# The second expert handled is always number 1, with token groups of 4, 2, 2 tiles and features in natural order

## The chip, the cores and the metric

The kernel runs on one core of one Trainium2 chip. The core has five engines that work side by side, each on its own list of instructions: TensorE (PE, with its weight loads shown apart as PEld), VectorE (DVE), ScalarE (ACT), GpSimd (POOL) and SyncE (SP), which here issues most DMAs. The metric is the device time of one execution in microseconds (us), the median of several runs.

## What is computed

One layer of a decoder with 1024 tokens of 1024 features: two attentions that share an input projection, a cross-attention to a memory of 256 rows, and a mixture of 16 experts in 4 groups of 4. Only the end of it is changed, so only that stands here:

```python
x = x + MemoryCrossAttention(RMSNorm(x), mem)
h = RMSNorm(x)                                    # gain moe_norm_g
g_sel = argmax(softmax(h @ w_group))              # one of 4 groups
aff = sigmoid(h @ w_expert) of that group         # 4 affinities
local = top_k(aff + expert_bias, 2)               # two experts of the group
w_sel = p_group * a_sel / sum(a_sel)
for e in range(16):
    act = silu(h @ w_gate[e]) * (h @ w_up[e])
    y = y + combine[:, e] * (act @ w_down[e])
x = x + y
```

Each token goes to two experts, so the 16 experts have 2048 tokens in all, unevenly spread.

## The kernel before

Tokens lie in 8 tiles of 128. The tiles of `x` stay in SBUF (`xres`), with eight more columns per token for weights, expert number and token number. `Memory.step` runs the memory attention as a pipeline over the tiles, beside the last half of the product with `w_out`: `E` adds the attention to `x`, `F` normalizes the tile for the experts (two ScalarE scalings L482, one VectorE product with the gain L484 that also reorders the features), `G` ends the router's logits and calls `Route.step`.

`Route.group` routes four tiles at a time in some 40 small VectorE steps. Its result is a place in a table in DRAM for each token and each of its two experts; a GpSimd indirect DMA (L197) then scatters 128 rows of 1032 floats to the table `d_xs`, eight DMAs per group. So there are two groups, of tiles 0 to 3 and 4 to 7. The table has 1280 rows for each expert.

Experts are handled in an order of ranks. Expert 0 has rank 0. After the first group, `Route.lead` finds the expert with most tokens so far (the lead, rank 1) and the one with least (rank 15); their numbers are written to `nb`, and L1669 loads both into registers of SP, before the loads of the lead's weights. The first 128 rows of expert 0 and of the lead are computed early: `lift` sets the base of these two for the second group to at least 128, so that their first 128 rows are complete after the first group. After the second group, `Route.places` sorts the other experts by tokens into ranks 2 to 14.

Each rank has a fixed number of rows, its room, for which the program is written out:

```python
ORDER_ = (0, 1, 15, 2, 8, 3, 9, 4, 10, 5, 11, 6, 12, 7, 13, 14)
ROOM = 2 * (256,) + 2 * (224,) + 2 * (192,) + 2 * (160,) + 5 * (128,) + 3 * (96,)
```

`ORDER_` is the order in which ranks are handled. For each, `moe` gathers the rows (L1682), transposes them on TensorE (L1718), loads the weights (gate and up L1733, down L1756), splits each into a high and a low part (L1747, L1748), multiplies, and adds the result to the output with an indirect DMA that skips rows without a token (L1765). `places` also counts, per rank, the blocks of 128 rows beyond the room (`cb`, in `nb[32:48]`) and their sum (`nb[48]`). At the end all engines load that sum (L1903) and, where it is over zero (L1904), run loops over the ranks (L1914) with an inner loop over the blocks beyond the room (L1917): these gather the rows, load that expert's weights again and multiply in plain f32.

The order of instructions on each engine comes from a scheduler in the build; DMAs of one queue start in its order. `issue_after` in the code holds an instruction behind another in that order.

The lines are those of the profile:

Of the kernel before, what the change touches and what calls it, by code (L numbers as in the profile page):

```python
# [22 lines left out]
NE = 16  # L23
# [9 lines left out]
class Route:  # L33
# [3 lines left out]


    GROUPS = ((0, 4), (4, 8))

    def __init__(self, K, rt, rows):
        self.K, self.rt = K, rt
        nc = K.nc
        V, G = nc.vector, nc.gpsimd
        til = lambda sh, nm, dt=F32: rt.tile(sh, dt, name=nm)
        self.til = til
        self.lg = til([128, T, 20], "lg")
        self.bias = K.row('moe_expert_bias', 0, 16, "e_bias", rt)
# [19 lines left out]
        self.base = til([128, 3, 16], "base")  # L68
        G.tensor_scalar(self.base[:, 0], self.iot, float(EXP), None, op0=OP.mult)

        self.lift = til([128, 16], "lift")
        G.tensor_copy(self.lift, self.base[:, 0])
        G.memset(self.lift[:, 0:1], 128.0)
        self.nb = til([1, 64], "nb", I32)
        self.todo, self.hold, self.puts, self.late = [], False, [], []

    def step(self, t):
        for a, b in self.GROUPS:
            if t == b - 1:
                self.todo.append(self.group(a, b))  # L80
        if t == T - 1:
            self.hold = False
            self.pump(10 ** 6)
# [9 lines left out]

    def group(self, t0, t1):
        K, til0 = self.K, self.til
# [4 lines left out]
        def til(sh, nm, dt=F32):  # L100
            return self.rt.tile(sh, dt, name=nm)
# [82 lines left out]

        pos, tmp, pc, ix = til([128, n, 16], "pos"), til([128, n, 2, 16], "tmp16"), til([128, n, 2], "pc"), til([128, n, 2], "ix", I32)
        V.tensor_add(pos, pre[:, 0:w].rearrange("p (t e) -> p t e", e=16), self.base[:, t0 // 4:t0 // 4 + 1].to_broadcast([128, n, 16]))
        yield
# [3 lines left out]
        yield  # L191
        self.last_ix = V.tensor_copy(ix, pc)
        yield

        for t in range(n):
            for z in range(2):
# [4 lines left out]
                if t0 >= EARLY:  # L201
                    self.late.append(q)
        V.tensor_add(self.base[:, t1 // 4], self.base[:, t0 // 4], pre[:, 128:144])
        if t1 == LEAD_AT:
            self.lead()
        if t1 == EARLY:
            V.tensor_tensor(self.base[:, t1 // 4], self.base[:, t1 // 4], self.lift, op=OP.max)

    def lead(self):
# [3 lines left out]
        own, e = til([128, 2, 16], "lown"), til([128, 2], "le")  # L213
        V.tensor_sub(key, self.base[:, LEAD_AT // 4], self.base[:, 0])
        V.scalar_tensor_tensor(key, key, 16.0, self.w16, op0=OP.mult, op1=OP.add)
        for i, (far, op) in enumerate(((-1.0, OP.max), (65536.0, OP.min))):
            V.tensor_scalar(key[:, 0:1], key[:, 0:1], 0.0, far, op0=OP.mult, op1=OP.add)
            V.tensor_reduce(m, key, AX.X, op)
            V.tensor_scalar(own[:, i], key, m, None, op0=OP.is_equal)
            V.tensor_mul(num, own[:, i], self.iot)  # L220
            V.tensor_reduce(e[:, i:i + 1], num, AX.X, OP.add)
        V.tensor_copy(self.nb[:, 0:2], e[0:1])
        self.le = e
        V.scalar_tensor_tensor(self.lift, own[:, 0], 128.0, self.lift, op0=OP.mult, op1=OP.add)
        self.shift = til([128, 16], "lshift")
        V.tensor_sub(self.shift, own[:, 0], own[:, 1])

    def places(self, lp):
# [4 lines left out]
        key, cnt = til([128, 16], "key"), self.til([128, 16], "cnt")  # L233
        V.tensor_sub(cnt, self.base[:, T // 4], self.base[:, 0])
# [32 lines left out]
class Memory:  # L267
# [6 lines left out]
    def __init__(u, K, x, mc, wq, quarter, route, cl):  # L274
# [28 lines left out]

        u.g_o = mc.tile([128, D], F32, name="g_o")
        for h in range(2):
            raw = K.wraw.tile([128, 512], F32, name="wr")
            src = I['moe_norm_g']
            nc.sync.dma_start(raw, bass.AP(tensor=src.tensor, offset=src.offset + 512 * h, ap=[[0, 128], [1, 512]]))
            G.tensor_copy(u.g_o.rearrange("p (c i) -> p c i", c=8)[:, :, 64 * h:64 * h + 64], raw.rearrange("p (i c) -> p c i", c=8))
        u.wor, u.wr0 = mc.tile([128, 2, 2, 20], F32R, name="w_o_router"), wr  # L310
# [188 lines left out]
class Hybrid:  # L499
# [41 lines left out]

    def newton(self, v, shape):

        nc, n = self.nc, shape[-1]
        s, y, t = (self.sm.tile([128, 17], dt, name=nm)[:, :n] for nm, dt in (("rq_s", I32), ("rq_y", F32), ("rq_t", F32)))
        nc.vector.tensor_scalar_add(v, v, EPS)
        nc.vector.tensor_scalar(s, v.bitcast(I32), 1, None, op0=OP.logical_shift_right)
# [1106 lines left out]
    def moe(self, route):  # L1654
# [13 lines left out]
        nb = route.nb  # L1668
        lead = [nc.values_load(nb[0:1, i:i + 1], engines=SP, min_val=0, max_val=NE - 1) for i in range(2)]  # L1669
        flat = lambda p, nm, dt=F32: p.tile([128, 2048], dt, name=nm)  # L1670
# [25 lines left out]
        def rows_of(loaded, exf, eT, early=False):  # L1696
# [139 lines left out]
        hB = early(1, lead[0], route.le[:, 0:1])  # L1836
        xg_ = [flat(r1, f"xg{i}") for i in range(2)]

        expert, loaded = [0, lead[0], lead[1]], {}

# [8 lines left out]
        def tokens(k):  # L1851
            n, exf = loaded[k][0], (0.0, route.le[:, 0:1])[k] if k < 2 else route.ex[:, ORDER_[k]:ORDER_[k] + 1]
# [45 lines left out]
        with ExitStack() as c:  # L1898
# [5 lines left out]
            with tc.If(nov > 0):  # L1904
# [7 lines left out]
                for a, b, room in runs:  # L1912
                    r = room // 128
                    with tc.For_i(a, b, 1) as s_:  # L1914
                        ne = nc.values_load(nb[0:1, ds(s_ + 32, 1)], min_val=0, max_val=9 - r)
                        ex = nc.values_load(nb[0:1, ds(s_ + 16, 1)], min_val=0, max_val=NE - 1)
                        with tc.For_i(0, ne, 1) as k:  # L1917
# [20 lines left out]
                            for h in range(2):  # L1938
                                p = self.tp().rearrange("p (a b) -> p a b", a=4)
                                for i in range(4):  # L1940
                                    nc.tensor.transpose(p[:, i, :], g0[:, tk(4 * h + i)], self.ident)
                                V.tensor_copy(gT[:, 4 * h:4 * h + 4], p)
# [53 lines left out]
```

## Time and profile before

| what | value |
|---|---|
| median of 3 runs | 1391.09 us (1387.9 to 1392.69) |
| the profiled execution's own time | 1394.23 us |
| its span, first to last instruction | 1392.5 us |
| mean granted clock of TensorE, share of full | 0.951 |
| busy: PE, DVE, ACT, POOL | 1233.7, 954.7, 792.9, 412.1 us |
| chain that ended last, by engine | PE 44%, DVE 19%, ACT 13%, DMA 13%, issue 7% |

Busy is the time in which an engine executes; the chain is followed back from the last instruction through what released each step. Shares over the whole span mix stages with different limits. The memory attention and router end at about 1108 us, the experts take the rest.

### The profile page before, as it was taken

To read this page: it belongs to the slowest core of one execution; us is meant where nothing else is said; L and a number is where in the kernel's file an instruction comes from. 1 tells how busy PE (TensorE), PEld (TensorE's weight loads), DVE (VectorE), ACT (ScalarE), POOL (GpSimd) and SP (SyncE) were. 2 spreads that over 40 slices of the span, in tenths; PEclk is the share of its full clock that TensorE was granted. 3 is DMA by queue.
4 is the path that set the end of the run, shared out by engine and by line. 5 is a ranking of instruction groups with operands and counts; after the bars stand their busy time and mean duration, and the time that the engine had idled before them with its cause. 6 is when DMAs were issued, how large, how long until landed. Compare 5 with 4: busy or idle time off the path is not lost.

```text
span 1392.5 us, 20692 instructions
## 1 busy us (share of the span) xinstructions
PE 1233.7 (89%) x6852; PEld 1032.6 (74%) x6853; DVE 954.7 (69%) x1983; ACT 792.9 (57%) x1651; POOL 412.1 (30%) x521
## 2 busy tenths in 40 slices
PE   3998999998899999999988999999989378999894
PEld 2877778777687778787777777887878256888772
DVE  6886956899999488878978465132367735677661
ACT  4654656887662477779988221043455335676652
POOL 4565100648774010011333222021223431011111
PEclk9999999999899999999999999998999689999987
DMA  7565003543435445345221244431121757899972
GB/s 206 159 199 148 12 24 101 163 131 124 135 116 174 151 133 185 139 167 164 65 82 55 83 136 126 174 86 38 34 78 73 286 215 232 272 344 299 284 219 37
DMA packets 145558, 203.55 MB, mean 146 GB/s; under 512 B 69632, under 2 KB 90880, under 8 KB 145440
## 3 DMA queue, kind: packets, MB, share of 16 engines
q1 hardware_dynamic: 134944, 172.57, 38.5%
q0 software_dynamic: 7440, 24.71, 6.6%
q10 hardware_dynamic: 3056, 4.84, 0.9%
q8 instruction: 56, 0.92, 0.3%
q14 instruction: 62, 0.51, 0.1%
HBM read 134.61 MB, written 69.70 MB: 147 GB/s over the span
## 4 chain that ended last, share of the span: by engine, by line
PE 44%; DVE 19%; ACT 13%; DMA 13%; issue 7%; POOL 2%; SPq 1%; DVEq 0%; ACTq 0%; POOLq 0%
PE acc L530 6%; PE acc L532 5%; PE acc L531 5%; PE s L530 3%; PE s L531 3%; PE s L532 3%; DMA gu_raw<-in_moe_w_gate_dram 2%; DMA gu_raw<-in_moe_w_up_dram 2%; ACT tk_junka L1222 2%; DVE ik_hi L1212 2%; PE s L955 2%; DVE ik_lo L1212 2%; DMA out_dram<-ey,etok 2%; PE tp L1378 1%; DVE PT_lo L517 1%
## 5 line engine op out<-in xcount | busy, mean ns | idle before, releaser
L522 POOL TENSOR_TENSOR wl<-wr,wh 128x512 fp32r<-128x512 f32 (+1 forms) x78 | 101.5, 1319 | 166.5 <-ACT wh L521 125.2
L517 DVE TENSOR_TENSOR PT_lo<-tp,PT_hi 128x512 fp32r<-128x512 f32 (+1 forms) x152 | 96.9, 656 | 23.3 <-ACT PT_hi L516 21.7
L530 PE MATMUL s<-hT_hi,wh 128*128 128x512 f32 x256 | 103.5, 404 | 3.4 <-ACT s L1083 3.4
L532 PE MATMUL s<-hT_hi,wl 128*128 128x512 f32 x256 | 102.8, 403 | 1.7 <-POOL wl L522 1.7
L531 PE MATMUL s<-hT_lo,wh 128*128 128x512 f32 x256 | 102.4, 402 | 0.0
L1765 POOL DMA_INDIRECT out_dram<-ey,etok x24 | 39.4, 1642 | 207.2 <-ACT ey L1780 57.3
L1748 DVE TENSOR_TENSOR gu_lo<-gu_raw,gu_hi 128x1024 fp32r<-128x1024 f32 x60 | 71.8, 1221 | 40.3 <-ACT gu_hi L1747 39.7
L516 ACT ACTIVATE PT_hi<-tp 128x512 fp32r<-128x512 f32 (+1 forms) x152 | 83.5, 572 | 23.4 <-PE tp L1378 9.8
L1222 ACT ACTIVATE tk_junka<-sc,tk_b 128x512 bf16<-128x512 f32 (+2 forms) x96 | 79.4, 827 | 30.5 <-DVE tk_b L1219 29.6
L521 ACT ACTIVATE wh<-wr 128x512 fp32r<-128x512 f32 (+1 forms) x78 | 46.7, 619 | 73.9 <-PE acc L532 26.7
L1747 ACT ACTIVATE gu_hi<-gu_raw 128x1024 fp32r<-128x1024 f32 x60 | 62.2, 1057 | 45.5 <-DMA gu_raw<-in_moe_w_gate_dram 21.9
L532 PE MATMUL acc<-wh,hT_lo 128*128 128x512 f32 (+2 forms) x240 | 85.5, 356 | 0.4 <-DVE hT_lo L517 0.4
L530 PE MATMUL acc<-wh,hT_hi 128*128 128x512 f32 (+2 forms) x240 | 85.3, 356 | 0.3 <-ACT hT_hi L516 0.2
L531 PE MATMUL acc<-wl,hT_hi 128*128 128x512 f32 (+2 forms) x240 | 84.3, 352 | 0.0
L1358 DVE TENSOR_REDUCE low<-s 128x1 f32<-128x256 f32 (+3 forms) x64 | 49.0, 769 | 21.3 <-PE s L1357 20.9
L530 PE MATMUL s<-eT1h,gu_hi 128*128 128x224 f32 (+2 forms) x192 | 54.0, 281 | 8.0 <-DVE ewt L1711 3.9
L530 PEld LDWEIGHTS s<-hT_hi,wh 128*128 128x128 f32 x256 | 49.8, 195 | 13.9 <-ACT s L1083 4.2
L532 PEld LDWEIGHTS s<-hT_hi,wl 128*128 128x128 f32 x256 | 49.9, 195 | 12.0 <-POOL wl L522 2.1
L964 DVE SCALAR_TENSOR_TENSOR sc<-rel,iw,sc 128x384 f32<-128x384 f32 (+5 forms) x42 | 43.4, 1034 | 21.2 <-ACT rel L958 18.0
L531 PEld LDWEIGHTS s<-hT_lo,wh 128*128 128x128 f32 x256 | 50.0, 195 | 10.4
L1360 ACT ACTIVATE P<-s,low 128x256 f32<-128x256 f32 (+3 forms) x64 | 48.1, 752 | 11.9 <-DVE low L1358 9.1
L530 PE MATMUL acc<-wh,mg_hi 128*128 128x512 f32 x128 | 52.0, 411 | 3.1 <-issue 3.1
(549 smaller groups left out, 4093.6 us busy)
## 6 DMA issues: line engine op xcount, KB each, us to landing
d_xs<-zero SPq DMA_DIRECT2D x32, 516.0 KB
dn_raw<-in_moe_w_down_dram SPq DMA_DIRECT2D x32, 512.0 KB
gu_raw<-in_moe_w_gate_dram SPq DMA_DIRECT2D x30, 512.0 KB
gu_raw<-in_moe_w_up_dram SPq DMA_DIRECT2D x30, 512.0 KB
wr<-in_w_in_dram SPq DMA_DIRECT2D x48, 256.0 KB
d_g<-s SPq DMA_DIRECT2D x32, 256.0 KB
gt<-d_g SPq DMA_DIRECT2D x16, 512.0 KB
xg<-d_xs SPq DMA_DIRECT2D x13, 512.0 KB
```

What stands on the lines that cost most here:

```text
L516: q = self.nc.scalar.activation(hi, src, AF.Copy)
L517: self.nc.vector.tensor_sub(lo, src, hi.bitcast(F32))
L522: self.nc.gpsimd.tensor_sub(lo, src, hi.bitcast(F32))
L530: mm(out, a[0], b[0], start=start, stop=False)
L531: mm(out, a[0], b[1], start=False, stop=False)
L532: mm(out, a[1], b[0], start=False, stop=stop)
L1212: V.tensor_scalar(junks[0][:, :(t + 1) * 128], blk(t), b[:, i:i + 1].bitcast(F32), None, op0=op, op1=OP.add, accum_out=cnt[:, i:i + 1])
L1222: A.activation(junka[:, :(t + 1) * 128], blk(t), AF.Sign, bias=b[:, i:i + 1].bitcast(F32), accum_out=cnt[:, i:i + 1])
L1358: nc.vector.tensor_reduce(low[:, b:b + 1], sp[:, 0:nch, 0:w], AX.XY, OP.min)
L1360: nc.scalar.activation(p_[:, :Wd].rearrange("p (a b) -> p a b", a=nch), sp[:, 0:nch, 0:w], AF.Exp, bias=low[:, b:b + 1], scale=-1.0, accum ...
L1747: A.activation(hi[:, z], raw_z, AF.Copy)
L1748: E.tensor_sub(lo[:, z], raw_z, hi[:, z].bitcast(F32))
```

## The change

The second expert handled is number 1, whatever the router finds; its weights' addresses are constants, so their loads need no register. `lead` now finds only the expert with least tokens, experts 0 and 1 apart. `places` gives expert 1 rank 1 by adding 65536 to its key. The room of each rank and the order of ranks are as before. Routing goes in three groups, of four, two and two tiles. The normalized rows keep the features in natural order: `F` is one VectorE instruction with the gain row as it lies in DRAM, and the transposes of the gathered rows pick every eighth feature. The reciprocal root of tiles 6 and 7 is made by Newton steps on VectorE (12 instructions) in place of GpSimd's power.

```diff
-    GROUPS = ((0, 4), (4, 8))
+    GROUPS = ((0, 4), (4, 6), (6, 8))
...
-        G.memset(self.lift[:, 0:1], 128.0)
+        for e in range(2):
+            G.memset(self.lift[:, e:e + 1], float(e * EXP + 128))
...
-        for i, (far, op) in enumerate(((-1.0, OP.max), (65536.0, OP.min))):
-            V.tensor_scalar(key[:, 0:1], key[:, 0:1], 0.0, far, op0=OP.mult, op1=OP.add)
-            V.tensor_reduce(m, key, AX.X, op)
...
+        V.tensor_scalar(key[:, 0:2], key[:, 0:2], 0.0, 65536.0, op0=OP.mult, op1=OP.add)
+        V.tensor_reduce(m, key, AX.X, OP.min)
...
-        V.tensor_scalar(key[:, 0:1], key[:, 0:1], 131072.0, None, op0=OP.add)
-        V.scalar_tensor_tensor(key, self.shift, 65536.0, key, op0=OP.mult, op1=OP.add)
+        for e in range(2):
+            V.tensor_scalar(key[:, e:e + 1], key[:, e:e + 1], 131072.0 - 65536.0 * e, None, op0=OP.add)
+        V.scalar_tensor_tensor(key, self.own, -65536.0, key, op0=OP.mult, op1=OP.add)
...
-        u.g_o = mc.tile([128, D], F32, name="g_o")
-        for h in range(2):
...
-            G.tensor_copy(u.g_o.rearrange("p (c i) -> p c i", c=8)[:, :, 64 * h:64 * h + 64], raw.rearrange("p (i c) -> p c i", c=8))
+        u.g_o = K.row('moe_norm_g', 0, D, "g_o", mc)
...
-        K.rsqrt(u.d.pop(('ms2', t)), (128, 1), out=y)
-        xn = u.ap.tile([128, D], F32, name="mxn", bufs=1)
-        for h in range(2):
-            m = slice(512 * h, 512 * h + 512)
-            nc.scalar.activation(xn[:, m], u.x[:, t, m], AF.Copy, scale=y)
-        nat = lambda v: v.rearrange("p (i c) -> p c i", c=8)
-        nc.vector.tensor_mul(u.x[:, t, 0:D].rearrange("p (c i) -> p c i", c=8), nat(xn), u.g_o.rearrange("p (c i) -> p c i", c=8))
+        (K.newton if t >= 6 else K.rsqrt)(u.d.pop(('ms2', t)), (128, 1), out=y)
+        xt = u.x[:, t, 0:D]
+        nc.vector.scalar_tensor_tensor(xt, xt, y, u.g_o, op0=OP.mult, op1=OP.mult)
...
-                x = xg[0:m, b // 128].rearrange("p (c i) -> p c i", c=KD)
+                x = xg[0:m, b // 128].rearrange("p (i c) -> p c i", c=KD)
...
-                            for q in (route.last_act, route.last_ix):
+                            for q in (route.last_act, route.last_ix[-1]) if h else route.last_ix[-2:-1]:
...
-        gu1 = gate_up(1, lead[0], (0,), V) + gate_up(1, lead[0], (1,), V)
+        gu1 = gate_up(1, 1, (0, 1), V)
...
-        dn1 = down(1, lead[0])
+        dn1 = down(1, 1)
+        expert.append(nc.values_load(nb[0:1, 1:2], engines=SP, min_val=0, max_val=NE - 1))
```

On SP, at the end of the memory attention, the queue before loads expert 0's down weights (`dn_raw`), then the register from `nb`, then the lead's gate and up weights (`gu_raw`), then the early rows (`d_xs`):

```order
L1756 DMA dn_raw<-in_moe_w_down_dram 128x1024 x2
L1669 TENSOR_LOAD nb
L1669 ISA x2
L1669 TENSOR_LOAD nb
L1669 ISA x2
L1733 ISA
L1733 DMA gu_raw<-in_moe_w_gate_dram 128x1024
L1733 ISA
L1733 DMA gu_raw<-in_moe_w_up_dram 128x1024
```

and the same place now:

```order
L1745 DMA dn_raw<-in_moe_w_down_dram 128x1024 x2
L1722 DMA gu_raw<-in_moe_w_gate_dram 128x1024
L1722 DMA gu_raw<-in_moe_w_up_dram 128x1024
L1722 DMA gu_raw<-in_moe_w_gate_dram 128x1024
L1722 DMA gu_raw<-in_moe_w_up_dram 128x1024
L1847 TENSOR_LOAD nb
L1847 ISA x2
L1722 ISA
L1722 DMA gu_raw<-in_moe_w_gate_dram 128x1024
L1722 ISA
L1722 DMA gu_raw<-in_moe_w_up_dram 128x1024
L1671 DMA dn_raw<-d_xs 128x1024
```

The second expert's four gate and up loads stand ahead of the register load; behind it comes the first half of the third expert's.

On POOL, at the end of the router, the roots of the tiles' mean squares (`mms` to `my`) and the scatters (`d_xs`) stand before as

```order
L538 TENSOR_SCALAR mms_11237<-mms_11237 128x1
L539 TENSOR_TENSOR my_11322<-mms_11237,mhalf 128x1
L197 DMA d_xs<-xres,ix 20480x1032 x8
L538 TENSOR_SCALAR mms_11318<-mms_11318 128x1
L538 TENSOR_SCALAR mms_11393<-mms_11393 128x1
L539 TENSOR_TENSOR my_11400<-mms_11318,mhalf 128x1
L539 TENSOR_TENSOR my_11447<-mms_11393,mhalf 128x1
```

and the same place now, where the last four scatters follow after the small MEMSETs of `room`, as the last eight did before:

```order
L527 TENSOR_SCALAR mms_11101<-mms_11101 128x1
L528 TENSOR_TENSOR my_11228<-mms_11101,mhalf 128x1
L527 TENSOR_SCALAR mms_11221<-mms_11221 128x1
L528 TENSOR_TENSOR my_11303<-mms_11221,mhalf 128x1
L198 DMA d_xs<-xres,ix_11341 20480x1032 x8
L198 DMA d_xs<-xres,ix_11515 20480x1032 x4
```

The roots of the last two tiles are gone from behind the first eight scatters, and four scatters of the second group stand there.

On DVE, between the second group's places (`ix`) and the last group's first steps, there stands now

```order
L193 CAST ix_11515<-pc 128x4
L1737 TENSOR_TENSOR gu_lo_11679<-gu_raw,gu_hi_11678 128x1024 x2
L541 SCALAR_TENSOR_TENSOR rq_t<-rq_t,mms_11371 128x1
L542 SCALAR_TENSOR_TENSOR my_11458<-rq_t,my_11458 128x1
L484 TENSOR_SCALAR lg<-lg,my_11458 128x20
L473 SCALAR_TENSOR_TENSOR xres<-xres,my_11458,g_o 128x1024
L111 TENSOR_REDUCE mx<-lg 128x2
```

Two splits of the second expert's weights (`gu_lo`) stand ahead of the end of tile 7's Newton steps; before, all four stood behind the last cast to `ix`.

## Rows read from the trace of the kernel before

**Rows 1.** Busy time by engine in four stretches; then PEclk, DMA share, GB/s.

```profile
1083.00:1108.00 25.00, 6.03 (x42) 5.17 (x42) 16.39 (x73) 9.23 (x15) 10.32 (x44) 0.63 0.88 328
1108.00:1131.00 23.00, 16.08 (x63) 12.12 (x61) 10.47 (x25) 5.38 (x8) 13.72 (x19) 0.80 0.89 332
1090.00:1100.00 10.00, 0.00 (x0) 0.00 (x0) 5.01 (x19) 4.81 (x8) 4.15 (x7) 0.50 1.01 382
1160.00:1260.00 100.00, 92.92 (x584) 79.36 (x583) 69.34 (x134) 67.25 (x104) 15.93 (x10) 0.97 0.94 307
```

**Rows 2.** Chain of waits, 1060 to 1140 us: start us, us, what.

```profile
1083.27 1.13 POOL d_xs L197
...
1108.05 1.79 POOL d_xs L197
...
1118.79 12.12 DMA d_xs<-xres,ix
...
1131.51 3.53 DMA emore<-d_xs
...
1135.36 1.94 PE tp L1718 x8
```

**Rows 3.** VectorE in order of time: start, us, instruction, idle before and releaser.

```profile
1094.50 0.23 DVE L495 TENSOR_SCALAR lg<-lg,my 128x20 f32<-128x20 f32 x1 [5.75 <-POOL mms L538]
```

**Rows 4.** Queue of loads in order of time, 1085 to 1134 us.

```profile
1088.23 0.70 SPq L1733 DMA_DIRECT2D gu_raw<-in_moe_w_gate_dram  x1
...
1103.90 0.34 SPq L1682 DMA_DIRECT2D dn_raw<-d_xs  x1
```

**Rows 5.** Instructions of L482, L484, L1748: ns min/median/max, first and last start us.

```profile
L482 ACT ACTIVATE mxn<-xres,my x16: 706/710/724, 1027.1 to 1099.1; 128x512 f32<-128x512 f32 x16
...
L484 DVE TENSOR_TENSOR xres<-mxn,g_o x8: 1908/2048/3157, 1029.1 to 1101.4; 128x1024 f32<-128x1024 f32 x8
...
L1748 DVE TENSOR_TENSOR gu_lo<-gu_raw,gu_hi x60: 1208/1219/1228, 1107.7 to 1352.7; 128x1024 fp32r<-128x1024 f32 x60
```

**Rows 6.** The same of L1718, weight loads of the row transposes.

```profile
L1718 PEld LDWEIGHTS tp<-ident,xg x176: 133/140/231, 1135.3 to 1347.7; 128*128 128x128 f32 x104, 96*128 96x128 f32 x40, 64*128 64x128 f32 x16, 32*128 32x128 f32 x16
```

**Rows 7.** DMA queue q0, four stretches: 1159.85-1171.14, 1179.72-1192.17, 1362.84-1369.81, 1369.81-1373.78 us. Packets, MB, share.

```profile
q0 software_dynamic: 144, 0.45, 20.3%
...
q0 software_dynamic: 144, 0.39, 16.1%
...
q0 software_dynamic: 144, 0.52, 49.7%
...
q0 software_dynamic: 48, 0.01, 2.0%
```

**Rows 8.** Instructions of the tail, L1903, L1904, L1991: ns min/median/max, starts.

```profile
L1903 DVEq TENSOR_LOAD <-nb x1: 541/541/541, 1370.4 to 1370.4; - x1
...
L1904 PEldq EVENT_SEMAPHORE  x2: 51/51/51, 1375.0 to 1375.2; - x2
...
L1904 POOLq COMPARE_BRANCH  x1: 53/53/53, 1380.9 to 1380.9; - x1
...
L1904 POOLq EVENT_SEMAPHORE  x6: 17/30/43, 1383.8 to 1385.6; - x6
...
L1904 POOLq INC_SWDGE_SEM  x1: 1291/1291/1291, 1385.7 to 1385.7; - x1
...
L1991 POOLq EVENT_SEMAPHORE  x4: 17/17/17, 1391.7 to 1392.4; - x4
...
L1991 POOLq DRAIN  x3: 46/103/4568, 1387.1 to 1392.2; - x3
```

**Rows 9.** L1765, the adding scatters: us from issue to landing.

```profile
DMA to landing us min/median/max: 3.2/7.4/10.7
```

**Rows 10.** Chain of waits, 1050 to 1060 us: plain f32 matmuls.

```profile
1055.62 1.44 PE acc L461 x12
```

**Rows 11.** ScalarE in order of time, 1119 to 1123 us.

```profile
1119.52 1.28 ACT L1806 ACT_TABLE_LOAD   x1
```

More of the change, by code (lines that the diff above doesn't have):

```diff
@@ L66, in __init__ @@
         G.memset(self.onesb, 1.0)
-        self.base = til([128, 3, 16], "base")
+        self.base = til([128, len(self.GROUPS) + 1, 16], "base")
         G.tensor_scalar(self.base[:, 0], self.iot, float(EXP), None, op0=OP.mult)
@@ L72, in __init__ @@
         G.tensor_copy(self.lift, self.base[:, 0])
-        G.memset(self.lift[:, 0:1], 128.0)
+        for e in range(2):
+            G.memset(self.lift[:, e:e + 1], float(e * EXP + 128))
         self.nb = til([1, 64], "nb", I32)
-        self.todo, self.hold, self.puts, self.late = [], False, [], []
+        self.todo, self.hold, self.puts, self.late, self.last_ix = [], False, [], [], []
     def step(self, t):
-        for a, b in self.GROUPS:
+        for i, (a, b) in enumerate(self.GROUPS):
             if t == b - 1:
-                self.todo.append(self.group(a, b))
+                self.todo.append(self.group(i, a, b))
         if t == T - 1:
@@ L92, in pump, with group @@
             self.hold = r == 2 and n < 10 ** 5
-    def group(self, t0, t1):
+    def group(self, gi, t0, t1):
         K, til0 = self.K, self.til
@@ L100, in til @@
         def til(sh, nm, dt=F32):
-            return self.rt.tile(sh, dt, name=nm)
+            return self.rt.tile([128, 4, *sh[2:]], dt, name=nm)[:, 0:n]
+        base = self.base
         l4, l16 = self.lg[:, t0:t1, 0:4], self.lg[:, t0:t1, 4:20]
@@ L183, in group @@
         yield
-        pos, tmp, pc, ix = til([128, n, 16], "pos"), til([128, n, 2, 16], "tmp16"), til([128, n, 2], "pc"), til([128, n, 2], "ix", I32)
-        V.tensor_add(pos, pre[:, 0:w].rearrange("p (t e) -> p t e", e=16), self.base[:, t0 // 4:t0 // 4 + 1].to_broadcast([128, n, 16]))
+        pos, tmp, pc, ix = til([128, n, 16], "pos"), til([128, n, 2, 16], "tmp16"), til([128, n, 2], "pc"), til([128, n, 2], f"ix{gi}", I32)
+        V.tensor_add(pos, pre[:, 0:w].rearrange("p (t e) -> p t e", e=16), base[:, gi:gi + 1].to_broadcast([128, n, 16]))
         yield
@@ L191, in group @@
         yield
-        self.last_ix = V.tensor_copy(ix, pc)
+        self.last_ix.append(V.tensor_copy(ix, pc))
         yield
@@ L202, in group, with lead @@
                     self.late.append(q)
-        V.tensor_add(self.base[:, t1 // 4], self.base[:, t0 // 4], pre[:, 128:144])
+        V.tensor_add(base[:, gi + 1], base[:, gi], pre[:, 128:144])
         if t1 == LEAD_AT:
-            self.lead()
+            self.lead(base[:, gi + 1])
         if t1 == EARLY:
-            V.tensor_tensor(self.base[:, t1 // 4], self.base[:, t1 // 4], self.lift, op=OP.max)
-    def lead(self):
+            V.tensor_tensor(base[:, gi + 1], base[:, gi + 1], self.lift, op=OP.max)
+    def lead(self, upto):
         V, til = self.K.nc.vector, self.til
         key, m, num = til([128, 16], "lkey"), til([128, 1], "lmx"), til([128, 16], "lnum")
-        own, e = til([128, 2, 16], "lown"), til([128, 2], "le")
-        V.tensor_sub(key, self.base[:, LEAD_AT // 4], self.base[:, 0])
+        self.own, e = til([128, 16], "lown"), til([128, 1], "le")
+        V.tensor_sub(key, upto, self.base[:, 0])
         V.scalar_tensor_tensor(key, key, 16.0, self.w16, op0=OP.mult, op1=OP.add)
-        for i, (far, op) in enumerate(((-1.0, OP.max), (65536.0, OP.min))):
-            V.tensor_scalar(key[:, 0:1], key[:, 0:1], 0.0, far, op0=OP.mult, op1=OP.add)
-            V.tensor_reduce(m, key, AX.X, op)
[L219 to L226, printed above, removed]
+        V.tensor_scalar(key[:, 0:2], key[:, 0:2], 0.0, 65536.0, op0=OP.mult, op1=OP.add)
+        V.tensor_reduce(m, key, AX.X, OP.min)
+        V.tensor_scalar(self.own, key, m, None, op0=OP.is_equal)
+        V.tensor_mul(num, self.own, self.iot)
+        V.tensor_reduce(e, num, AX.X, OP.add)
+        V.tensor_copy(self.nb[:, 1:2], e[0:1])
     def places(self, lp):
@@ L233, in places @@
         key, cnt = til([128, 16], "key"), self.til([128, 16], "cnt")
-        V.tensor_sub(cnt, self.base[:, T // 4], self.base[:, 0])
+        V.tensor_sub(cnt, self.base[:, len(self.GROUPS)], self.base[:, 0])
         V.scalar_tensor_tensor(key, cnt, 16.0, self.w16, op0=OP.mult, op1=OP.add)
-        V.tensor_scalar(key[:, 0:1], key[:, 0:1], 131072.0, None, op0=OP.add)
-        V.scalar_tensor_tensor(key, self.shift, 65536.0, key, op0=OP.mult, op1=OP.add)
+        for e in range(2):
+            V.tensor_scalar(key[:, e:e + 1], key[:, e:e + 1], 131072.0 - 65536.0 * e, None, op0=OP.add)
+        V.scalar_tensor_tensor(key, self.own, -65536.0, key, op0=OP.mult, op1=OP.add)
         gt, oh, ex = (til([128, 16, 16], nm) for nm in ("gt", "oh", "ex"))
@@ L302, in __init__ @@
             G.tensor_add(u.two, u.two, K.ident[0:40, 20 * e:20 * e + 20])
-        u.g_o = mc.tile([128, D], F32, name="g_o")
-        for h in range(2):
-            raw = K.wraw.tile([128, 512], F32, name="wr")
-            src = I['moe_norm_g']
-            nc.sync.dma_start(raw, bass.AP(tensor=src.tensor, offset=src.offset + 512 * h, ap=[[0, 128], [1, 512]]))
-            G.tensor_copy(u.g_o.rearrange("p (c i) -> p c i", c=8)[:, :, 64 * h:64 * h + 64], raw.rearrange("p (i c) -> p c i", c=8))
+        u.g_o = K.row('moe_norm_g', 0, D, "g_o", mc)
         u.wor, u.wr0 = mc.tile([128, 2, 2, 20], F32R, name="w_o_router"), wr
@@ L540, in rsqrt, with newton @@
         return y
-    def newton(self, v, shape):
+    def newton(self, v, shape, out=None):
         nc, n = self.nc, shape[-1]
         s, y, t = (self.sm.tile([128, 17], dt, name=nm)[:, :n] for nm, dt in (("rq_s", I32), ("rq_y", F32), ("rq_t", F32)))
+        y = y if out is None else out
         nc.vector.tensor_scalar_add(v, v, EPS)
@@ L1668, in moe @@
         nb = route.nb
-        lead = [nc.values_load(nb[0:1, i:i + 1], engines=SP, min_val=0, max_val=NE - 1) for i in range(2)]
         flat = lambda p, nm, dt=F32: p.tile([128, 2048], dt, name=nm)
@@ L1833, in moe @@
         dn = down(0, 0)
-        gu1 = gate_up(1, lead[0], (0,), V) + gate_up(1, lead[0], (1,), V)
+        gu1 = gate_up(1, 1, (0, 1), V)
         hA = early(0, 0, 0.0)
-        hB = early(1, lead[0], route.le[:, 0:1])
+        hB = early(1, 1, 1.0)
         xg_ = [flat(r1, f"xg{i}") for i in range(2)]
-        expert, loaded = [0, lead[0], lead[1]], {}
+        expert, loaded = [0, 1], {}
         def load(k):
@@ L1851, in tokens @@
         def tokens(k):
-            n, exf = loaded[k][0], (0.0, route.le[:, 0:1])[k] if k < 2 else route.ex[:, ORDER_[k]:ORDER_[k] + 1]
+            n, exf = loaded[k][0], float(k) if k < 2 else route.ex[:, ORDER_[k]:ORDER_[k] + 1]
             return n, rows_of(loaded[k], exf, [cut(w, n) for w in eT[k % 2]])
         rest = first_small(128, gu, hA)
-        dn1 = down(1, lead[0])
+        dn1 = down(1, 1)
+        expert.append(nc.values_load(nb[0:1, 1:2], engines=SP, min_val=0, max_val=NE - 1))
         nb = route.places(r3)
@@ L1940, in moe @@
                                 for i in range(4):
-                                    nc.tensor.transpose(p[:, i, :], g0[:, tk(4 * h + i)], self.ident)
+                                    nc.tensor.transpose(p[:, i, :], g0[:, 0:D].rearrange("p (i c) -> p c i", c=KD)[:, 4 * h + i], self.ident)
                                 V.tensor_copy(gT[:, 4 * h:4 * h + 4], p)
```

## The prediction

> **What bounds the kernel now.** I read the busy times of stretches first. They show one hole. From 1083 to 1108 us TensorE is busy 6.0 us of 25, at a mean granted clock of 0.63, and from 1108 to 1131 16.1 us of 23, while the DMA engines are at shares of 0.88 and 0.89 [rows 1]. Later, from 1160 to 1260, TensorE is busy 92.9 us of 100 with the DMA share at 0.94: two resources near their limits, little to win. Next the chain of waits, for what the hole is made of: the first scatter of token rows at 1083.27, the first of the second eight at 1108.05, the last at 1118.79, landed 12.12 us later, a gather of 3.53 us, transposes at 1135.36 [rows 2]. So the path there is router, scatter, landing, gather. Then the engines' order of time. `VectorE` stands idle 5.75 us before 1094.50, because the rsqrt of the last two tiles is on GpSimd behind eight scatters [rows 3]. On the queue of loads the second expert's gate and up weights start at 1088.23, as its number is computed from the first four tiles, and the early gather starts at 1103.90 [rows 4]. Last I read the tail, because the program ends in a block for experts with more tokens than room that the kernel before skips (L1904). That block decides this forecast.
>
> **The router stage.** By rows 1 the 48 us from 1083 to 1131 move 25 x 328 + 23 x 332 GB/s = 15.8 MB. The second expert's gate and up weights, four DMAs of 0.52 MB or 2.1 MB, leave that stretch: they now follow the first expert's loads, ahead of the register load that waited for the router. At the stretch's own rate that is 2.1/0.33 = 6.4 us; where all the holes closed too (13.7 MB at the 382 GB/s of its best 10 us [rows 1], 36 us), 12 us. The last two tiles' rsqrt goes to VectorE, 24 instructions as small as the one in rows 3, 0.2 us each, among the router's, against the wait of 5.75 us. The second group's scatters are cut in two: four start behind the first eight, so only four, not eight, follow the router's last result: the first and the eighth start 10.74 us apart [rows 2], so four steps of 1.5 us, 6 us, go. But two gu_lo instructions of 1.22 us [rows 5] now stand on VectorE ahead of the last group, and behind them queue all its router steps. These gains overlap, since the bytes still have to flow. I take -10 us, bounds -3 (only the four scatters' issue, less the two gu_lo) and -18 (wait, issue and bytes all on the path). What is late next is the landing of the last four scatters, then the gather of 3.53 us.
>
> **Natural order of features.** Per tile two ScalarE scalings of 0.71 us and a strided VectorE multiply of 2.05 us become one contiguous VectorE instruction; nearest row, two f32 inputs of 128x1024: 1.22 us [rows 5]. That is 1.42 + 2.05 - 1.22 = 2.25 us per tile. Eight tiles give 18 us of engine time, mostly beside TensorE's work in the memory attention. I take -3, little more than one tile's share for the stretch ahead of the first scatter; bounds 0 (all covered) and -5 (two tiles). In return the 192 transposes of gathered rows (176, and 16 of the early blocks) read weights 8 floats apart. The trace has no such load: now one takes 140 ns [rows 6]. VectorE's ratio in rows 5, 2.05/1.22 = 1.7, would make it 100 ns longer, and at most 192 x 0.10 = 19 us; the load runs beside matmuls, so the lower bound is 0. I take +3, near the lower, as TensorE's transposes are spread over the DMA-bound stage. The Trainium skill ("SBUF — State Buffer", in "Door 1: The DMA port swizzle") says consecutive accesses are at full bandwidth only within one 16-byte line, so a stride of 32 bytes pays on each access. Rows 5 agree for VectorE; by that rule on every transpose the term would be 19 us instead of 3.
>
> The rest I cost at nothing: the counting base with one more slot, and the lead search with one branch instead of two are VectorE instructions of 0.2 us on 16 columns, hidden by the scatters; the two strided gain copies on GpSimd fall in the w_out stage, where it waits. Uncovered they are 2 us, of either sign.
>
> **The overflow.** Each rank in the order of handling has fixed rows, `ROOM`: 256, 256, 224, 224, 192, 192, 160, 160, five times 128, three times 96. What an expert has beyond is done by the block at the end. The trace gives each expert's tokens, because the adding DMA moves a row of 4096 bytes for each real token [rows 7]. In order: the lead's early block 0.45 MB and its second 0.39 MB, about 110 + 96 = 206 rows; the expert at rank 7 0.52 + 0.01 MB, 128 + 2. Working the reference's routing out on its inputs gives the same: number 2 (now the lead) 206, number 7 130, number 1 only 79. Now number 1 gets rank 1 and its room of 256, number 2 joins the sorted ranks at the front, and every expert between moves down one. Number 7 comes from rank 7, room 160, to rank 8, room 128, with 130 tokens. Two tokens overflow, `nov` is 1, and all five engines enter the block. All others fit (206 and 189 in 224; 179 and 157 in 192; 154 and 139 in 160; 127 in 128).
>
> The block has six loops with 16 turns in all over the ranks, one of them with an inner turn. A turn holds register loads (0.54 us each, two on VectorE), a compare, a chain of 12 semaphore waits (51 ns each on TensorE's queue), updates of the DMA semaphores on GpSimd, and between turns a drain and two barriers. No loop ran before, so I bound a turn by the end rows [rows 8]. Cheap: 1.1 + 0.6 + 0.8 for the barriers (the end block takes 0.8 us behind its drain) + branches, some 2.9 us. Dear: also two updates of 1.29 us, a GpSimd drain of 4.57 us and two taken jumps of 2.9 us (GpSimd's compare at 1380.9, its next instruction at 1383.8): 15.5 us. I take 6 us, nearer the cheap end, as the loops' code is short. 16 x 6 = 96 us, bounds 46 and 248.
>
> The inner turn is one serial chain: five small VectorE steps 1; zeroing scatter to landing 7.4 [rows 9]; 3.1 MB of weights at 307 GB/s [rows 1] 10.2, with the gather beside them; 32 plain f32 matmuls at twice 0.12 us [rows 10], since the granted clock is 0.50 while TensorE idles [rows 1], 7.7; table load 1.28 [rows 11] and two small steps, 2.1; four matmuls of 512 columns 3.8; two ScalarE copies 1.4; the adding scatter 7.4. Sum 41 us; bounds 27 (full clock, landings of 3.2) and 48 (landings of 10.7).
>
> The Trainium skill ("Runtime: NRT & Kernel Launch", "Instruction fetch mechanics") says a taken branch stalls only where its target lies outside the two instruction pages held, which trigger a fetch. The far jump in rows 8 agrees, 2.9 us on GpSimd; the short jumps of a turn no row shows. By that rule the turns are cheap: a rival below.
>
> **Sum.** Profiled execution 1394.23 us: -10 - 3 + 3 + 96 + 41 = +127, so 1521 us. The median of the runs is 1391.09, 3.1 below; on its scale 1518 us.
>
> **Rivals.** (1) Cheap turns: a turn is 2.9 to 4 us because every jump stays in held code. For it: short loops; a compare is 0.05 us in rows 8. Against: GpSimd's 4.57 us drain. 1391 - 10 + 16 x 3.3 + 35: about 1469. (2) Dear turns: the drain and a missed jump on one of five engines in most turns, all waiting for the slowest, 10 to 12 us: 1391 - 10 + 16 x 11 + 44: about 1601. (3) The other side: the block isn't entered, because the kernel's arithmetic or the ranks leave number 7 within 128. It decides at exactly two tokens. Then only the first terms are left: 1391 - 10 = 1381, faster. Against it: rows 7 show 128 + 2, so the kernel's own routing counts 130. (4) The change doesn't do what it says: the loads move in program order but wait for SBUF that the memory attention frees, and start at 1088 as before. The router term shrinks to -4 and the time is 1524; within the forecast.
>
> **How the numbers follow.** Forecast with turns of 4 to 10 us, (4) included: 0.70, its own range 1475 to 1585. Rival (1) 0.12, (2) 0.13, (3) 0.05. The range takes in the forecast and most of both neighbours: 1450 to 1605. A measurement of this kernel tells some 0.3% from no change (runs 1387.9 to 1392.69). Faster needs rival (3): 0.04, with 0.01 for the same, where the strided loads eat that gain; slower 0.95.
>
> **What would show it.** In the profile after: instructions of the overflow block's lines, one 0.01 MB adding scatter in it, 100 us or more with all engines nearly idle at the end; turns of equal length between barriers. For the stage: gu_raw loads beside the memory attention, no wait of VectorE for the GpSimd rsqrt, gather of the rest some 10 us earlier, strided transposes near 140 ns. No overflow rows at all would make the prediction wrong; so would turns that the scheduler or the hardware overlaps to under 3 us or stretches past 12.

## The result, and the profile after

The changed kernel takes 1501.8 us (median of 4 runs, 1499.08 to 1506.85) against 1389.68 before in the same comparison: 8.07% slower, ratio 1.0807 [1.0781, 1.0833]. The forecast was 1518 and the range 1450 to 1605. Its profiled execution took 1500.96 us, span 1499.1.

The overview of the page (busy tenths in 40 slices, 37.5 us each; then granted clock and DMA share) shows the new part at once: the last three slices are idle but for one.

```profile
PE   3998999988999999999989999999848998994030
...
PEclk9999999999999999999999999999979999998565
DMA  7464015444354444443123462112395898882020
```

The block for experts over their room, by lines of its loops on GpSimd (POOLq marks its branches, register loads and waits; ns min/median/max, first and last start us): the branch to the block, the loads of a turn's count in two stretches of time, and the drains and updates between turns.

```profile
L1894 POOLq COMPARE_BRANCH  x1: 40/40/40, 1375.5 to 1375.5; - x1
...
L1905 POOLq TENSOR_LOAD <-nb x9: 291/302/490, 1377.8 to 1425.8; - x9
...
L1905 POOLq TENSOR_LOAD <-nb x7: 283/294/307, 1461.1 to 1490.8; - x7
...
L1904 POOLq DRAIN  x20: 34/38/4561, 1382.2 to 1490.3; - x20
...
L1907 POOLq INC_SWDGE_SEM  x15: 154/169/1293, 1378.7 to 1491.5; - x15
```

Sixteen turns, as forecast. Nine start from 1377.8 to 1425.8 (6.0 us from one to the next on average, 10.0 from the first to the second), seven from 1461.1 to 1490.8 (4.95 us), and 35.3 us lie between, where the turn with work is. From the branch at 1375.5 to the end at 1499.1 are 123.6 us; before, from 1380.9 to 1392.5 [rows 8], 11.6. The difference is 112 us, the whole loss of the medians (the two profiled spans differ by 106.6, since the branch comes 5.4 us earlier here). The chain of waits of that one turn (start us, us, what):

```profile
1426.68 4.25 issue
...
1431.17 3.44 DMA d_xs<-o_zero,oix
...
1434.63 3.47 DMA og<-d_xs
...
1439.04 15.89 issue
...
1455.16 1.57 POOL out_dram L1754
```

The first 4.25 us are listed as issue, but GpSimd stands at the zeroing scatter in them and waits for VectorE's row numbers (`oix`):

```profile
1431.17 1.05 POOL L1915 DMA_INDIRECT d_xs<-o_zero,oix  x1 [53.66 <-DVE oix L1914]
```

VectorE's branch into the inner loop starts at 1427.2 us and its first step at 1430.24. Then come the zeroing scatter, the gather, and 15.9 us in which GpSimd waits for the matmuls and the small steps behind them; the matmuls stand in TensorE's order of time (start us, us, instruction, idle before):

```profile
1438.14 1.97 PE L1931 MATMUL tp<-ident,og 128*128 128x128 f32 x8 [70.66 <-DMA og<-d_xs]
1440.77 3.40 PE L1943 MATMUL s<-ogT,owg 128*128 128x128 f32 x16 [0.66 <-DMA owg<-in_moe_w_gate_dram]
...
1450.46 3.70 PE L1951 MATMUL acc<-owd,oa__15221 128*128 128x512 f32 x8 [0.93 <-DVE oa__15221 L1946]
```

The router stage, busy time by engine, granted clock, DMA share and GB/s, for [rows 1]:

```profile
1083.00:1108.00 25.00, 7.05 (x41) 5.50 (x40) 23.30 (x123) 4.67 (x8) 17.09 (x51) 0.61 1.01 382
1108.00:1131.00 23.00, 21.10 (x97) 16.63 (x98) 9.25 (x31) 9.83 (x15) 5.77 (x7) 0.97 0.59 208
```

The hole is now one stretch, and TensorE is busy 21.1 us of the second, where it was 16.1. The scatters and loads that changed, in order of time on GpSimd (the first, ninth and last scatter), SP and TensorE, for [rows 2 to 4]:

```profile
1079.53 1.12 POOL L198 DMA_INDIRECT d_xs<-xres,ix  x1 [3.43 <-DVE lkey L217]
...
1090.84 1.67 POOL L198 DMA_INDIRECT d_xs<-xres,ix  x1 [0.92 <-DVE ix L193]
...
1105.33 0.95 POOL L198 DMA_INDIRECT d_xs<-xres,ix  x1 [0.31 <-issue]
```

```profile
1047.25 0.33 SPq L1722 DMA_DIRECT2D gu_raw<-in_moe_w_gate_dram  x1
...
1095.40 0.34 SPq L1671 DMA_DIRECT2D dn_raw<-d_xs  x1
```

```profile
1122.02 1.13 PE L1707 MATMUL tp<-ident,xg 128*128 128x128 f32 x8 [0.54 <-DMA emore<-d_xs]
```

The second expert's loads start at 1047 instead of 1088, the ninth scatter at 1090.8 instead of 1108.1, and the transposes that open the expert stage at 1122.0 instead of 1135.4: 13.3 us earlier. Of these, 3.7 lie ahead of the first scatter (1079.5 against 1083.3), where executions with one and the same order of instructions differ by more, as a table below shows. But GpSimd's branch behind the last expert comes only 5.4 us earlier. For [rows 5, 6], the normalization and the strided weight loads:

```profile
L473 DVE SCALAR_TENSOR_TENSOR xres<-xres,my,g_o x8: 1271/1278/3246, 1024.4 to 1093.3; 128x1024 f32<-128x1024 f32 x8
...
L1707 PEld LDWEIGHTS tp<-ident,xg x176: 180/193/230, 1122.0 to 1345.2; 128*128 128x128 f32 x104, 96*128 96x128 f32 x40, 64*128 64x128 f32 x16, 32*128 32x128 f32 x16
```

### The profile page after: what moved, and what is told of

Its sections match the earlier page's. It is cut to its first block, busy times and chain, and to the rows that moved or that the text cites. A ratio compares the mean times of both kernels' runs of the same rounds, so it can differ in the third digit from the quotient of the medians.

```text
span 1499.1 us, 23751 instructions
## 1 busy us (share of the span) xinstructions
PE 1251.0 (83%) x6932; PEld 1048.6 (70%) x6933; DVE 953.9 (64%) x2055; ACT 784.9 (52%) x1640; POOL 413.6 (28%) x521
## 5 line engine op out<-in xcount | busy, mean ns | idle before, releaser
L520 PE MATMUL s<-eT1l,gu_hi 128*128 128x224 f32 (+2 forms) x192 | 56.9, 297 | 0.0
L521 PE MATMUL s<-eT1h,gu_lo 128*128 128x224 f32 (+2 forms) x192 | 56.0, 292 | 0.0
```

The lines of the kernel that those rows point to most:

```text
L520: mm(out, a[0], b[1], start=False, stop=False)
L521: mm(out, a[1], b[0], start=False, stop=stop)
```

## The experiments

Two questions: is the block the whole loss, and why do 13 us at the start of the expert stage come to so little at its end? Theory: the block costs 112 us, by its turns. Rivals: the change itself slows the stage; or the block has a fixed entry price. In the expectations, "the first job" and "the first kernel of this job" are x1_room. A kernel with "skip" in its name leaves out the two overflowing tokens' share of expert 7; it serves to price the block.

**Block not needed (x1_room).**

```diff
-ROOM = ... 2 * (160,) + 5 * (128,) + 3 * (96,)
+ROOM = ... 3 * (160,) + 4 * (128,) + 3 * (96,)
```

> The changed kernel with room 160 at rank 8 (was 128), so that expert 7 with its 130 tokens fits and the block at the end is not entered. Theory (the block is the whole loss, the stage before it gains): the trace of the changed kernel has 112 us between GpSimd's branch into the block and the end more than before, so 1502 less 112, about 1390, plus up to 1 for 32 more rows: 1385 to 1392. Rival (the slowdown comes in part from the three groups, the strided transposes or another order): the time stays above 1400.

Measured: 1400.6 us, ratio 1.0057 [1.0034, 1.0081]. The block is gone and 101 us with it, but the theory's 1392 is missed, and the rival's number, above 1400, is just met. My price of 1 us for a rank with room 160 was too low, as the next runs show; x9_skip shows that the rival's cause, the change itself, is not it.

**The same overflow in the kernel before (x2_before_room).**

```diff
-ROOM = ... 2 * (160,) + 5 * (128,) + 3 * (96,)
+ROOM = ... 1 * (160,) + 6 * (128,) + 3 * (96,)
```

> The kernel before with room 128 at rank 7 (was 160), its only edit: expert 7 now overflows there by its two tokens. Theory (one expert over its room costs the block's 16 turns and one inner turn, whatever else the kernel does): 1390 plus 112, about 1500 (1495 to 1505). Rival (the block is dear only in the changed kernel, by its strided transposes or code layout): under 1480.

Measured: 1491.71 us, ratio 1.0696 [1.0651, 1.0740]: the rival falls; the theory's range, 1495 to 1505, is missed by 3 us. Its branch into the block comes at

```profile
L1904 POOLq COMPARE_BRANCH  x1: 40/40/40, 1371.2 to 1371.2; - x1
```

9.7 us before that of the kernel before: a rank with room 128 has one block of rows in place of two. From branch to the end of its span of 1491.1 are 119.9 us, 108 more than the 11.6 of before. So the block costs nearly the same in the old kernel, and the room of this rank is worth some 10 us.

**Natural order undone, room 160 (x3_order).** Edit: gain row, `F` and transposes as on the minus lines of the diff.

> The first kernel of this job (room 160 at rank 8) with the natural order of features undone: gain row, normalization and transposes as before the change. Theory A (strided weight loads of the transposes, 193 ns against 140 in the traces, lie on TensorE's path in the expert stage): 176 of them by 53 ns are 9 us; the normalization costs 0 to 5 us more; 4 to 9 us faster than the first kernel. Theory B (the lead lost in the expert stage is due to the order of the experts' work and the clock): within 3 us of the first kernel.

Measured: 1404.15 us, 1.0076 [1.0047, 1.0106]: not faster than x1_room (2.6 us slower by the ratios, within theory B's 3). Theory A falls here.

**Five turns in place of 16 (x8_five_turns).**

```diff
-                for a, b, room in runs:
+                for a, b, room in [q for q in runs if q[2] == 128]:
```

> The changed kernel with the block at the end cut to the one loop over ranks 8 to 12 (room 128), which on these inputs holds the only expert over its room: five turns in place of 16. Theory (a turn costs the same 5.4 us whether it has work or not, measured in the trace): 11 turns by 5.4 are 59 us less, about 1443. Rival (the block costs a fixed entry, GpSimd's drain and first misses, and turns are cheap): less than 30 us saved, above 1472.

Measured: 1442.1 us, 1.0350 [1.0314, 1.0385]. The medians differ by 59.7 us for 11 turns, 5.4 us each. The branch comes at

```profile
L1894 POOLq COMPARE_BRANCH  x1: 45/45/45, 1386.3 to 1386.3; - x1
```

and the span ends at 1446.2: 59.9 us against 123.6, or 5.8 us for each of the 11 turns, the long first one among them; the ratios say the same. So the block goes by its turns, and the rival, a fixed entry with cheap turns, falls.

**The block skipped (x9_skip).** Every instruction of the change stays in its place; only the constant differs.

```diff
-            with tc.If(nov > 0):
+            with tc.If(nov > 1):
```

> The changed kernel with the block at the end entered only for more than one block beyond the room, so that it is skipped here; every instruction before it is the same. It leaves out the two overflowing tokens' share of expert 7. Theory A (the block costs 112, branch to end 123.6 in the trace of the changed kernel against 11.6 of before, and the 13 us that the expert stage starts earlier are nearly lost within it): 1387 to 1391. Theory B (the early start comes through and the block costs more than its trace shows): 1376 to 1382. Theory C (the first job's 1400.6 with a room of 160 shows a slowdown by the change itself): 1395 or more. A also says that the 160 row room, not the change, made the first job's kernel slow: two blocks of rows where one was, 10 us.

Measured: 1388.66 us, ratio 0.9985 [0.9967, 1.0002]: theory A. By the two ratios the block costs (1.0807 - 0.9985) x 1390 = 114 us, and the rest of the change is worth 2 us or nothing. x1_room against it: 10 us for the room by the ratios, as x2_before_room shows from the other side; x3_order against x10_skip_order below gives 14.

**Which part starts the stage earlier, and what is it worth?** Three kernels with the block skipped. x10_skip_order undoes the natural order as above. x11_skip_late:

```diff
+        V.tensor_scalar(self.nb[:, 0:1], e[0:1], 0.0, 1.0, op0=OP.mult, op1=OP.add)
...
-        gu1 = gate_up(1, 1, (0, 1), V)
+        one = nc.values_load(nb[0:1, 0:1], engines=SP, min_val=0, max_val=NE - 1)
+        gu1 = gate_up(1, one, (0, 1), V)
```

x13_skip_two_groups sets `GROUPS = ((0, 4), (4, 8))`.

> The same with the block skipped (two tokens' share left out), and the natural order of features undone. Theory A (the strided weight loads, 53 ns more each, are what eats the early start): 176 by 0.053 is 9 us faster than the kernel without this edit, less 0 to 5 for the dearer normalization. Theory B (they lie beside matmuls and cost nothing; the two orders differ only by what the scheduler makes of them): within 4 us of it, or slower.

> The block skipped (two tokens' share left out), and the address of the second expert's gate and up weights taken from a register that is loaded after the router's first group, as before the change, though its value is always 1. Theory A (the early loads are what starts the expert stage earlier): first transposes of gathered rows 5 to 10 us later than the 1122 of the changed kernel, and the end 0 to 4 us later. Theory B (the three groups and the Newton roots start it earlier, the loads were hidden): transposes within 3 us of 1122.

> The changed kernel with the block skipped (two tokens' share left out) and two token groups, 0 to 3 and 4 to 7, in place of three. Theory A (the early start of the stage comes from the cut of the second group: the ninth scatter starts at 1087 instead of 1108): ninth scatter some 10 us or more later, first transposes at 1127 or later, and the end within 3 us of 1388.7, as the late loads gave. Theory B (it comes from the loads and the roots; the groups don't matter): transposes within 3 us of 1119 to 1122.

The starts (us) are those of each kernel's profiled execution; the first scatter is that of token rows, the length goes from the first transposes to the last adding scatter:

| kernel | ratio to before | first scatter | first transposes | last adding scatter | scatter to transposes | length |
|---|---|---|---|---|---|---|
| before | 1 | 1083.3 | 1135.4 | 1380.1 | 52.1 | 244.8 |
| after (ahead of the block) | 1.0807 [1.0781, 1.0833] | 1079.5 | 1122.0 | 1374.7 | 42.5 | 252.7 |
| x8_five_turns (ahead of the block) | 1.0350 [1.0314, 1.0385] | 1086.2 | 1133.6 | 1385.5 | 47.4 | 251.9 |
| x9_skip | 0.9985 [0.9967, 1.0002] | 1075.6 | 1119.1 | 1373.4 | 43.5 | 254.2 |
| x10_skip_order | 0.9977 [0.9959, 0.9995] | 1077.6 | 1121.3 | 1371.6 | 43.7 | 250.3 |
| x11_skip_late | 1.0004 [0.9983, 1.0025] | 1076.9 | 1126.2 | 1371.2 | 49.4 | 245.0 |
| x13_skip_two_groups | 0.9983 [0.9962, 1.0004] | 1076.7 | 1124.1 | 1380.2 | 47.5 | 256.1 |

The kernels after, x8_five_turns and x9_skip have the same order of instructions up to the block. Their first scatters still lie up to 10.6 us apart and their first transposes 14.5: so much do single executions differ, and no smaller difference of absolute times in two profiles tells kernels apart. Within an execution the numbers repeat better: 42.5 to 47.4 us from the first scatter to the transposes, where before has 52.1 (and x2_before_room and x15_before_gather_later, with the same order up to there, 51.5 and 51.6), and a length of 251.9 to 254.2, where before has 244.8. So, counted from the first scatter, the stage starts 4 to 10 us earlier by the change, not 13, and it is 7 to 9 us longer.

x10: theory B, 1.3 us with overlapping intervals; the strided loads cost nothing that can be measured. x11: the transposes come 7 us later than in x9_skip (4 later than the 1122 that the expectation names) and 49.4 us after the first scatter, outside the spread above; the time by the ratios is 2.6 us longer. That is theory A as far as one execution tells. x13: between its theories; the ninth scatter starts at 1096.2 (9 us later than the 1087.0 of x9_skip, still 12 earlier than before), the transposes 5 us later but 47.5 us after the first scatter, at the edge of the spread; the end is the same by the ratios. So the early loads move the start of the stage, the cut of the groups perhaps, and no start moves the end by as much. The Newton roots were not taken out by themselves.

**Is it the gather in the queue of loads (x14_skip_gather_later, x15_before_gather_later)?** In x9_skip SP stands at two gathers for 18.5 us, of which one wait is 17.6, with weight loads behind them (start us, us, instruction):

```profile
1236.22 1.05 SPq L1745 DMA_DIRECT2D dn_raw<-in_moe_w_down_dram  x2
1237.51 18.51 SPq L1671 DMA_DIRECT2D xg<-d_xs  x2
1256.22 0.87 SPq L1676 DMA_DIRECT2D emore<-d_xs  x2
1257.34 0.33 SPq L1722 DMA_DIRECT2D gu_raw<-in_moe_w_gate_dram  x1
```

and the DMA share is 0.57 there:

```profile
1240.00:1260.00 20.00, 17.64 (x115) 14.72 (x114) 10.80 (x22) 11.16 (x19) 3.64 (x3) 0.91 0.57 156
```

```diff
-                load(i + 2)
                 gu1 = gate_up(i + 1, expert[i + 1], (0,))
...
             dn = down(i, expert[i], V)
+            if i + 1 < NE:
+                load(i + 2)
```

> The changed kernel with the block skipped (two tokens' share of expert 7 left out), and in the loop over experts the gather of rows for the expert after next is issued behind the next expert's gate and up loads and this expert's down loads on the queue of loads, not ahead of them. Theory A (the early start is given back because this gather waits up to 18.5 us for a buffer that the transposes free, with weight loads queued behind it, and the DMA share falls to 0.57 from 1240 to 1260): no such wait over 10 us, and the time 4 to 8 us below the 1388.7 of the kernel without this edit, 1380 to 1385. Theory B (the expert stage is bound by TensorE and bytes, and whatever starts earlier is lost at another place): within 3 us of 1388.7. Theory C (the gather comes too late for its own transposes): over 1392.

> The kernel before with the same move of the gather. Its longest such wait is 9.2 us and its DMA share stays at 0.9 or over in the middle of the stage. Theory A: 0 to 3 us faster than before, since there is less to win. Theory C: slower by 3 or more. If A holds here with more than 4 us it is a version that beats both kernels.

Measured: x14 1392.99 us, 0.9995 [0.9975, 1.0015]; x15 1400.37 us, 1.0060 [1.0039, 1.0080]. In x14 the wait is gone and stands at another place. SP's waits of 1130 to 1350 us (us in total, times, longest):

```profile
SPq L1722 <- DVE gu_lo L1737: 42.4, 11, 10.2
SPq L1671 <- PE tp L1707: 18.1, 5, 7.5
```

The waits for transposes (`tp`) come to 18.1 us there; in x9_skip they were

```profile
SPq L1671 <- PE tp L1707: 73.5, 12, 17.6
```

My theory A falls: the wait went, and the time did not fall. By the median, 1392.99, theory C's number is just met, by the ratio, 1.4 us over x9_skip with overlapping intervals, theory B's. In x11_skip_late, too, these waits come to 73.5 us, and its stage is short. For x15 theory C holds.

**A version that keeps the choice of the lead (x17_lead_kept).** Three groups, natural order and Newton roots, with `lead`, its registers and `places` as before the change, so that nobody overflows and all is computed.

> The changed kernel with the choice of the second expert as before the change (the one with most tokens after four tiles, its weights by a register), so that three groups, natural order and Newton roots stay and no expert is over its room; it computes everything. Theory A (these parts start the expert stage 7 to 10 us earlier and the stage gives it back, as with the block skipped and late loads, 1391.4): within 0.3% of before, 1387 to 1394. Theory B (the parts are worth their early start where the expert order is the old one): 1380 to 1385, a version that beats both.

Measured: 1387.41 us, 0.9977 [0.9954, 1.0000]: theory A. First transposes at 1128.7, last adding scatter at 1371.9: length 243.2. Its median is the lowest of the kernels here that compute everything, by 0.2%, just at the edge of what can be told.

**A version for number 1 (x12_one_block).** Room 128 at rank 1 without the second block's code, and room 160 at rank 8.

> A version that may beat both: the changed kernel with room 128 for number 1 (it has 79 tokens, so its second block of 128 rows, with gather, transposes, 24 + 12 matmuls, is left out) and room 160 at rank 8, so that no expert here is over its room and the block at the end is general still. From about 1390 for the change without overflow: 10 more for the room of 160, 15 less for the block (24 by 0.41 and 12 by 0.41 us of matmuls): 1383 to 1388. Rival (the stage is bound by its weight loads, so matmuls left out save nothing): 1395 or more.

Measured: 1514.14 us, 1.0885 [1.0851, 1.0918]. A miss of my own reading: `lift` sets number 1's rows of the later groups to start at row 128, so its count is 128 and what the last four tiles bring, over the room of 128 although it has 79 tokens. The block was entered again, and its long turn was the second, rank 1.

## Why the prediction came out as it did

- **The overflow, the step that decides: right.** Number 7 overflows by two tokens, `nov` is 1, 16 turns with one inner turn. 137 us were forecast, 112 (trace) to 114 (ratios) measured. The block's own 123.6 us replace the 11.6 of the old end.
- **The turn: 6 us forecast, 5.4 measured**, 87 us for 16 in place of 96. That it came so near is in part luck, as 6 was chosen between two bounds and is no sum. The dear bound fell because GpSimd's drain takes 4.56 us only the first time, then a median 0.04, and the semaphore update 1.29 us once, then a median 0.17. Rival 1 was too cheap: it took the chain of 12 waits once, at some 0.05 us a wait. In the trace GpSimd's waits start 0.09 us apart, and some turns have two chains, of 1.1 us each. The turns are not of equal length, either: behind the first most take 4.1 to 4.7 us and four take 6.8 to 7.4. In three of the four, one or two engines start nothing for 2.4 to 2.7 us behind a branch (GpSimd at 1402.9, ScalarE at 1414.3, SP and ScalarE at 1479), and in the fourth a branch of TensorE takes 1.58 us. So pauses like the missed jumps of rival 2 are there, but in four turns of 15, not in most. What the engines do in them, the trace does not show.
- **The inner turn: 41 forecast, 31 measured** (35.3 us from its start to the next turn's, less 4.6 for a turn without work). Three terms were some 4 us too dear: the zeroing took 3.44 us and the adding scatter 3.4 to its landing, the near end of [rows 9], not 7.4, where next to no other DMA was under way (DMA share 0.03 from 1378 to 1431 us, 0.01 behind 1457); and the first matmuls started 6.1 us after the gather's start, not 10.2, as they waited for the gate weights alone. Against that, VectorE's late entry into the inner loop, some 3 us, stood in no term. The matmuls came nearly as sized: 8.8 us for the first 32 against 7.7, and 3.70 us for the last ones against 3.8.
- **Router stage, -10: failed as a term, right as a mechanism.** Loads, scatters and gather came earlier as described (the expert stage by 13.3 us in the two profiles, 4 to 10 counted from the first scatter, inside the bounds), but I took the start of the next stage for the end of the program. With the block skipped all of the change is worth 2 us or nothing.
- **Rival 4 (loads not early): false.** They start at 1047.
- **Natural order: +3 and -3, measured as nothing.** The multiply takes 1.28 us, near the 1.22 forecast. The strided weight load takes 193 ns, 53 more than before, where I wrote "near 140" for the test; 176 by 53 ns are 9 us of weight loads, and x10_skip_order gets back 1.3.
- The sum: 23 us too much for the block (137 against 114 by the ratios), less 8 too much gain for the stage, are 15; with the base of 1391.09 in place of 1389.68 they make the 16 by which 1518 lies above 1501.8. The two errors work against each other, so the time came nearer than its terms.

The lines behind the turn: three pieces of a chain of waits (start us, us, what), and TensorE's branches (ns min/median/max).

```profile
1423.26 0.04 POOLq L1907
1423.31 0.04 issue
1423.35 0.05 POOLq L1907
```

```profile
L1907 PEldq COMPARE_BRANCH  x48: 78/181/1579, 1368.1 to 1493.5; - x48
```

What stays open is why the stage gives the start back. What the runs show: where the second expert's weights are loaded early (after, x8, x9, x10, x13, x14) the stage is 250 to 259 us long; where they wait for a register (before, x11, x17) it is 243 to 245. TensorE's order of transposes and matmuls in the stage is nearly the same in the three late ones (99% of its pieces, matched in order, agree with before) and another in the early ones (70% agree, 81% in x14), though the change edits next to nothing there: the scheduler makes it. In x15_before_gather_later the weights wait for the register, yet the order is another (69%) and the stage 256.7 us long; so a long stage does not need the early loads, though there the moved gather is a cause of its own. That the order is the cause is argued, not shown; holding TensorE's order fixed was not tried.

## What to carry to other kernels

A table of rooms and the order that fills it are one thing: move one expert up and all between move down, and the one that was near its edge goes over. Count rows at every rank, with the kernel's own numbering (the rows that `lift` skips count). A dynamic loop that normally does not run costs by its turns, not by its work: here some 81 of the block's 123.6 us were the 15 turns that found nothing. And a gain ahead of a stage is worth what the end of that stage shows; measure it with the later fault switched off by one constant. Before two starts in two profiles are compared, see how far apart they lie in executions with the same order of instructions.

## What the runs showed of the hardware

- Strided f32 weight loads of TensorE (8 floats apart): a median of 193 ns against 140 for contiguous ones of the same shapes (after and before).
- A turn of a dynamic loop over five engines: 4.1 to 7.4 us without work, from one of GpSimd's loads to the next, but 10.0 for the first, which holds a drain of 4.56 us against a median 0.04 later.
- A rank with room 160 in place of 128 costs some 10 us (by the ratios 10 in x1_room against x9_skip and 14 in x3_order against x10_skip_order; 9.7 to the branch in x2_before_room), though only 32 rows are added: the second block has its own transposes, down matmuls and adding scatter. That these are the cause is not shown: the stage's length differs by 12 and 8 us in the last two pairs (262.1 and 250.3; 236.6 and, before, 244.8), but by 0.8 in the first (255.0 and 254.2), whose other time lies ahead of the stage.
